# A transformer block in split fp32: seven-product blocks in two more places of the MLP, two quarters of a gate moved beside them, its first loads moved forward

## The chip, the cores and the metric

The kernel runs on one core of a Trainium2 chip. The time is that of one execution on the device in microseconds (us), from the first to the last instruction and what lies around them. Lower is better. Names used below: PE is TensorE (matrix products), PEld its weight loads, DVE is VectorE, ACT ScalarE, POOL GpSimd, SP the engine that issues most of the loads.

## The reference

One layer is computed for 128 context tokens and 256 latent tokens, 384 in all, at width 2048:

```python
shift_a, scale_a, gate_a, shift_f, scale_f, gate_f = mod     # silu(cond) @ ada_w + ada_b, cond is c_ctx or c
h = rmsnorm(x, norm_w[0]) * (1 + scale_a) + shift_a
q, k, v, o, g, u = split(h @ w_in)
hm = rmsnorm(mlstm_bidir(q, k, v, g + gate_bias, C0, n0, m0)) * sigmoid(o)   # 8 heads x 128, chunks of 128
hp = pool_mixer(u)                                           # 4 groups x 256
x = x + gate_a * rmsnorm(concat(hm, hp) @ w_out, norm_w[1])
h = rmsnorm(x, norm_w[2]) * (1 + scale_f) + shift_f
y = square(relu(h @ w1)) @ w2                                # 2048 -> 8192 -> 2048
x = x + gate_f * rmsnorm(y, norm_w[3])
```

Outputs are y for both token groups and the final mLSTM state of the context scan.

## The kernel before, in words

All products are in fp32 made of three matmuls: each operand is split into a rounded part hi and the rest lo, and hi·hi, hi·lo and lo·hi are summed in one PSUM bank. A weight slab (128 x 1024 numbers, 512 KB) is loaded by SP (`load_w`, L119), ACT copies it to hi (L131), DVE subtracts to get lo (L132), PE multiplies (`mm3`, L140 to L142).

The stages follow each other on PE: adaLN products and the input projection (0 to 205 us), q/k with attention, gates and pooling beside them (to 430), o (to 490), w_out (to 630), the norm r1 and the vector gate_f's first part (to 641), and then the MLP in eight chunks of eight hidden tiles each. Beside the large products run generators that a `Feed` (L147) steps: each call of a feed adds its rate to a sum and takes one step of the generator when the sum reaches one. `gemm_T` (L163) calls its feeds once per weight slab. A planner orders PE, DVE and ACT instructions by what they wait for, in order of the program for equal ones; a few stretches are in written order (`manual_schedule`).

The six modulation vectors come from 2048 x 12288 weights `ada_w`. Some columns go through PE (`ada_mat`, L208: matmuls of 32 x 256), others through DVE (`ada_vec`, L252): 32 multiply-and-add instructions per 512 columns over slabs `ada_raw`, line L273 (the first pair L271), then a small matmul sums over partitions. In w_out the generator `mid_vec` (L681) does five vectors of 1024 columns in this way. gate_f (`gate_f`, L839) has its first quarter done by `ada_mat` in the stretch between w_out and w1, where PE would wait for the norm (`fill`, L859); half of those weights go through the tiles y0 and y1, which are not yet in use. Its other three quarters follow by `ada_vec` at rate RATE_GF beside chunks 0 and 1.

In the MLP a `w1_group` (L1148) makes two hidden tiles: 96 matmuls of 384 columns. They are evacuated by `evac_normed` (L810) or `evac_pair` (L818). Then w2 follows. There are two forms. `mlp_out` (L935) does a block of 512 output columns n with 8 hidden tiles x 3 token tiles x 3 matmuls = 72 matmuls of 512 columns. `mlp_seven` (L1060) does the same block with seven products in place of eight for each 2 x 2 block of (hidden tile, token tile) and column half, after Winograd's scheme: 132 matmuls of 256 columns for the block, for which `evac_pair` builds sums of hidden tiles (s, hs) and DVE sums and splits weight slabs (L1077 and L1107 to L1121). Two of the products go into sums of their own, r16 and r7, over the chunks, and `seven_done` (L1135) adds these to y at the end of chunk 6. Before the change chunks 2 to 6 are done by `mlp_seven`, chunks 0, 1 and 7 by `mlp_out`. The last block of chunk 7 and the final norm, gate and residual stand in `last_part` (L1035), with `done` (L1014) for the squares and the gate.

## Time and profile before

| | |
|---|---|
| median of 3 runs | 1716.28 us (1715.2 to 1723.14) |
| the profiled execution's own time | 1715.41 us |
| its span, first to last instruction | 1713.4 us |
| mean granted TensorE clock | 0.995 of 2.4 GHz |
| PE / DVE / ACT / POOL busy | 98% / 75% / 42% / 9% of the span |
| DMA | 320.88 MB, mean 187 GB/s |

All times of views below are those of the profiled execution, counted from its first instruction. A share of busy time is an average over stages: which engine sets the pace has to be read stage by stage, from the waits of PE and from windows.

### The profile page before, as it was taken

How to read it: one execution, taken by the hardware profiler on the slowest of the kernel's cores; microseconds unless marked ns; L12 is line 12 of the kernel's file. 1: busy time of each engine (PE TensorE's matmuls, PEld its weight loads, DVE VectorE, ACT ScalarE, POOL GpSimd, SP SyncE). 2: the span in 40 equal slices, each digit the busy share in tenths (PEclk: the TensorE clock that was granted, in tenths of full speed). 3: DMA queues.
4: the chain of work that ended last, by engine and by line, in shares of the span. 5: the costliest groups of instructions: out<-in, count | busy, mean ns of one | idle time of the engine just before them, and what ended most of it. 6: DMA issues, size and time to landing. Idle time of an engine off the chain costs nothing.

```text
span 1713.4 us, 27071 instructions
## 1 busy us (share of the span) xinstructions
PE 1673.3 (98%) x10661; PEld 1567.0 (91%) x10661; DVE 1284.6 (75%) x1900; ACT 721.9 (42%) x1178; POOL 150.3 (9%) x186
## 2 busy tenths in 40 slices
...
GB/s 301 306 278 282 295 145 261 235 238 238 220 232 268 260 275 143 208 173 181 213 172 123 148 136 121 139 131 112 152 126 112 158 121 113 161 108 98 265 137 106
DMA packets 255758, 320.88 MB, mean 187 GB/s; under 512 B 14368, under 2 KB 218768, under 8 KB 255248
## 3 DMA queue, kind: packets, MB, share of 16 engines
...
q8 instruction: 83, 1.36, 0.3%
...
HBM read 308.61 MB, written 10.51 MB: 186 GB/s over the span
## 4 chain that ended last, share of the span: by engine, by line
PE 85%; DVE 6%; DMA 5%; issue 2%; ACT 1%; SPq 1%; POOL 0%; DVEq 0%; ACTq 0%; POOLq 0%
PE acc_w L140 10%; PE acc_w L141 10%; PE acc_w L142 10%; PE y L932 4%; PE y L931 3%; PE y L933 3%; PE y L1089 3%; PE y L1090 3%; PE y L1088 3%; DVE ada_acc L273 2%; DMA raw_u<-in_w_in_dram 2%; PE acc_wo L140 2%; PE acc_wo L142 2%; PE acc_wo L141 2%; PE y_yz L1089 2%
## 5 line engine op out<-in xcount | busy, mean ns | idle before, releaser
L132 DVE TENSOR_TENSOR lo_w<-raw_w,hi_w 128x1024 fp32r<-128x1024 f32 x176 | 215.2, 1224 | 192.9 <-ACT hi_w L131 191.0
L141 PE MATMUL acc_w<-h2l,hi_w 128*128 128x384 f32 (+1 forms) x1024 | 345.6, 338 | 0.5 <-DVE h2l L887 0.5
L142 PE MATMUL acc_w<-h2h,lo_w 128*128 128x384 f32 (+1 forms) x1024 | 344.8, 337 | 0.0
L140 PE MATMUL acc_w<-h2h,hi_w 128*128 128x384 f32 (+1 forms) x1024 | 343.8, 337 | 1.1 <-ACT h2h L883 0.6
L131 ACT ACTIVATE hi_w<-raw_w 128x1024 fp32r<-128x1024 f32 x176 | 186.5, 1060 | 304.3 <-PE acc_w L141 97.2
L273 DVE SCALAR_TENSOR_TENSOR ada_acc<-ada_raw,sg,ada_acc 128x1024 f32<-128x1024 f32 (+1 forms) x240 | 258.8, 1116 | 1.3 <-DMA ada_raw<-in_ada_w_dram 1.3
L140 PEld LDWEIGHTS acc_w<-h2h,hi_w 128*128 128x128 f32 x1024 | 192.1, 188 | 2.7 <-ACT h2h L883 0.9
L141 PEld LDWEIGHTS acc_w<-h2l,hi_w 128*128 128x128 f32 x1024 | 192.6, 188 | 1.2 <-DVE h2l L887 0.8
L142 PEld LDWEIGHTS acc_w<-h2h,lo_w 128*128 128x128 f32 x1024 | 192.5, 188 | 0.1
L1076 ACT ACTIVATE hi_t<-w 128x1024 fp32r<-128x1024 f32 x80 | 84.4, 1061 | 87.2 <-PE y L1090 23.5
L1077 DVE TENSOR_TENSOR lo_t<-w,hi_t 128x1024 fp32r<-128x1024 f32 x80 | 97.4, 1223 | 11.7 <-ACT hi_t L1076 11.3
L1077 DVE TENSOR_TENSOR lo_b<-w,hi_b 128x1024 fp32r<-128x1024 f32 x60 | 73.3, 1222 | 35.3 <-ACT hi_b L1076 35.3
L1076 ACT ACTIVATE hi_b<-w 128x1024 fp32r<-128x1024 f32 x60 | 63.7, 1061 | 77.1 <-PE acc_w L141 51.3
L131 ACT ACTIVATE hi_wo<-raw_wo 128x1024 fp32r<-128x1024 f32 x32 | 34.1, 1064 | 75.2 <-DMA raw_wo<-in_w_out_dram 43.1
...
L226 PE MATMUL ada<-ada_raw,cT 128*32 128x256 f32 x672 | 47.6, 403 | 1.9 <-DMA ada_raw<-in_ada_w_dram 1.8
L399 PE MATMUL v<-hi_v,hh 128*128 128x384 f32 (+1 forms) x144 | 47.6, 332 | 0.0
L400 PE MATMUL v<-lo_v,hh 128*128 128x384 f32 (+1 forms) x144 | 46.5, 323 | 0.0
L401 PE MATMUL v<-hi_v,hl 128*128 128x384 f32 (+1 forms) x144 | 46.5, 323 | 0.0
L132 DVE TENSOR_TENSOR lo_wo<-raw_wo,hi_wo 128x1024 fp32r<-128x1024 f32 x32 | 40.2, 1270 | 7.3 <-ACT hi_wo L131 7.3
L140 PE MATMUL acc_k<-hh,hi_k 128*128 128x384 f32 x128 | 44.4, 347 | 1.2 <-ACT C L608 1.2
L140 PE MATMUL acc_q<-hh,hi_q 128*128 128x384 f32 x128 | 44.4, 347 | 0.0
...
## 6 DMA issues: line engine op xcount, KB each, us to landing
ada_raw<-in_ada_w_dram SPq DMA_DIRECT2D x188, 512.0 KB, 4.8
raw_w<-in_w_dram SPq DMA_DIRECT2D x176, 512.0 KB, 4.1
...
```

What stands on the lines that cost most here:

```text
L131: nc.scalar.activation(hi[:, 0:n], raw[:, 0:n], AF.Copy)
L132: low = lambda: nc.vector.tensor_tensor(lo[:, 0:n], raw[:, 0:n], hi[:, 0:n].bitcast(F32), op=ALU.subtract)
L140: nc.tensor.matmul(ps, lh, rh, start=start, stop=False)
L141: nc.tensor.matmul(ps, lh, rl, start=False, stop=False)
L142: mm3.ins = nc.tensor.matmul(ps, ll, rh, start=False, stop=stop).ins
L273: nc.vector.scalar_tensor_tensor(acc[:, g, :], raw[:, a, :], cj, acc[:, g, :], op0=ALU.mult, op1=ALU.add)
L931: nc.tensor.matmul(acc, xh[:, s], hi, start=k == 8 * ch, stop=False)
L932: nc.tensor.matmul(acc, xh[:, s], lo, start=False, stop=False)
L933: nc.tensor.matmul(acc, xl[:, s], hi, start=False, stop=k == 8 * ch + 7)
L1076: nc.scalar.activation(hi, raw, AF.Copy)
L1077: nc.vector.tensor_tensor(lo, raw, hi.bitcast(F32), op=ALU.subtract)
L1089: nc.tensor.matmul(acc, xh, wl, start=False, stop=False)
```

## The change

1. Chunk 1 goes by `mlp_seven` (S_FIRST 1), and so do the first two of the four blocks of chunk 7 (N_LAST 2). `evac_pair` serves all hidden tiles from 8 on. In chunk 7 the product x7's difference of hidden tiles is built by `evac_pair` as a tile d (one ACT copy and one more DVE subtraction per pair), and `seven_done` for the first two blocks runs as a feed beside the other two blocks.
2. Of gate_f's three `ada_vec` quarters one is left in chunk 0, at rate 0.4 in place of 0.65. The other two run beside chunks 1 and 2 at rate 0.25, with slabs of 256 KB and three buffers in place of 512 KB and four. `mlp_seven` steps the feed after each product of the second and third token tile.
3. Six of the eight loads for gate_f's first quarter go into y0, y1 and y2, and are issued during w_out (`early`). For this the MLP's pool is opened before w_out, and the pool of the ada slabs lies on the right side of SBUF.
4. The first chunk of the projection of u does all hi·hi, then all hi of the weight with lo of the tokens, then lo of the weight, and its weight's lo is subtracted after the token's lo.
5. The ACT copy `ada_sb` gets high priority. The Square of the head norm (L638) writes to an SBUF tile of its own in the cases where it wrote into a PSUM bank. The final gate is held in pieces of 384 columns. The buffers of z go from 5 to 4, the slots from 56 to 55, and the second raw pool's from 3 to 2.

```diff
-N_SLOT = 56
+N_SLOT = 55
 N_W = 4
 N_ADA = 4
 N_E = 1
 ADA_STEPS = (4, 0, 5, 0, 0)
 X_ORDER = "tatatatabtatatatat"
 N_X = 4
-RATE_GF = 0.65
-S_FIRST, S_LAST = 2, 6
+RATE_GF = 0.4
+RATE_GS = 0.25
+S_FIRST, S_LAST, N_LAST = 1, 6, 2
...
+                raw = raws.pop(0) if raws else None
+                if raw is None:
+                    raw = (wp if tag == "lo" else adap).tile([P, nj, w], F32, tag=tag, name=f"ada_raw_{i}_{k0}_{j0}", bufs=N_W if tag == "lo" else N_ADA)
+                    nc.sync.dma_start(raw, aw[:, j0:j0 + nj, c0:c0 + w])
...
-        sb = adap[0].tile([P, 512], F32, tag="adasb", name=f"ada_sb_{parts[0][0]}_{parts[0][1]}", bufs=1)
-        nc.scalar.activation(sb[:, 0:w], ps[:, 0:w], AF.Copy)
+        sb = adap.tile([P, 512], F32, tag="adasb", name=f"ada_sb_{parts[0][0]}_{parts[0][1]}", bufs=1)
+        with tc.high_priority():
+            nc.scalar.activation(sb[:, 0:w], ps[:, 0:w], AF.Copy)
...
+        acc = vec["acc"].tile([P, 2, n], F32, tag="adaacc", name=f"ada_acc_{i}_{c}", bufs=1)
+        c0, nj = i * D + c, vec["slab"] // n
 
         def load(t):
-            raw = adap[0].tile([P, nj, n], F32, tag="ada", name=f"ada_raw_{i}_{c}_{t}", bufs=N_ADA)
+            raw = vec["pool"].tile([P, nj, n], F32, tag="ada", name=f"ada_raw_{i}_{c}_{t}", bufs=vec["bufs"])
             nc.sync.dma_start(raw, aw[:, nj * t:nj * t + nj, c0:c0 + n])
             return raw
 
...
+            ways = ((0, 0), (1, 0), (0, 1))
+            for ps in [ways[n:n + 1] for n in range(3)] if s == ci == 0 else [ways]:
+                for k in range(nk):
+                    for i in range(3):
+                        for a, b in ps:
+                            nc.tensor.matmul(acc[i][:, 0:n], h[k0 + k][a][:, i * P:(i + 1) * P], (hi, lo)[b][:, k, :],
+                                             start=k == 0 and a + b == 0, stop=k == nk - 1 and b == 1)
+            if s == ci == 0:
+                w_first = load_chunk(0, 1, h_ins)
...
+                unread = (num if i > 0 else att.tile([P, 2, 129], F32, tag="num", name=f"sq_{hp}_{hl}", bufs=2))[:, 1, 0:128]
...
-                nc.scalar.activation(num[:, 1, 0:128] if i > 0 else ps[:, 260:388], hs[:, hl, :], AF.Square, accum_out=ssh[:, i, hd:hd + 1])
+                nc.scalar.activation(unread, hs[:, hl, :], AF.Square, accum_out=ssh[:, i, hd:hd + 1])
...
+    early = []
     for cols in ([0, 256], [512], [768], [1024], [1280], [1536], [1792]):
+        if cols[0] in (768, 1024, 1280):
+            for m in range(2):
+                n = len(early)
+                t = y[n // 2][:, 1024 * (n % 2):1024 * (n % 2) + 1024].rearrange("p (j c) -> p j c", c=256)
+                nc.sync.dma_start(t, aw[:, 4 * (n % 4):4 * (n % 4) + 4, 5 * D + 256 * (n // 4):5 * D + 256 * (n // 4) + 256])
+                early.append(t)
...
-        z = mlp.tile([P, NTOK], F32, tag="z", name=f"z{t}", bufs=5)
-        nc.scalar.activation(z, ps[:, 0:NTOK], AF.Relu)
+
+        z = relu_first(t, ps) if t < 10 else mlp.tile([P, NTOK], F32, tag="z", name=f"z{t}", bufs=4)
+        if t >= 10:
+            nc.scalar.activation(z, ps[:, 0:NTOK], AF.Relu)
         nc.scalar.activation(z, z, AF.Square)
         if t % 2 == 0:
             z_even.append(z)
             return
-        z0, s = z_even.pop(), mlp.tile([P, NTOK], F32, tag="z", name=f"s{t}", bufs=5)
+        z0, s = z_even.pop(), mlp.tile([P, NTOK], F32, tag="z", name=f"s{t}", bufs=4)
         a11, a21, a12, a22 = z0[:, P:2 * P], z0[:, 2 * P:], z[:, P:2 * P], z[:, 2 * P:]
         s1, s2, s4 = (s[:, i * P:(i + 1) * P] for i in range(3))
         tt = nc.vector.tensor_tensor
         tt(s1, a21, a22, op=ALU.add)
-        tt(a21, a11, a21, op=ALU.subtract)
+        if t < 8 * S_LAST + 8:
+            tt(a21, a11, a21, op=ALU.subtract)
+        else:
+            s3, d = mlp.tile([P, NTOK], F32, tag="z", name=f"d{t}", bufs=4), slot(f"hd{t}", F32R)
+            tt(s3[:, 0:P], a11, a21, op=ALU.subtract)
+            hi, lo = d[:, 0:P], d[:, P:2 * P]
+            nc.scalar.activation(hi, s3[:, 0:P], AF.Copy)
+            tt(lo, s3[:, 0:P], hi.bitcast(F32), op=ALU.subtract)
+            hid["d", t] = hi, lo
...
-        yield from ada_mat([(5, 0, 2), (5, 2, 2)], ("ada", None), [y[i][:, 1024 * n:1024 * n + 1024] for i in range(2) for n in range(2)])
+        yield from ada_mat([(5, 0, 2), (5, 2, 2)], raws=early)
         for q in (1, 2, 3):
-            yield from ada_vec(5, 512 * q, 512, adap[0])
+            yield from ada_vec(5, 512 * q, 512)
+            if q == 1:
+                vec["half"] = True
+                while vec["half"]:
+                    yield
...
+        for c, d in pieces:
+            lo, hi = max(a, c), min(b, d)
+            if lo < hi:
+                nc.vector.tensor_tensor(y[i][:, lo:hi], y[i][:, lo:hi], gf[min(i, 1), c][:, lo - c:hi - c], op=ALU.mult)
...
+                if m == "x7" and half and ch > S_LAST:
+                    xh, xl = hid["d", t + 1]
...
+            if tok:
+                for f in feeds:
+                    f()
...
     for ch in range(8):
         if ch < S_FIRST:
-            w1_group(4 * ch + 4, (ff, fx), 386 if ch == 0 else NTOK)
-            mlp_out(ch, (ff, fx, fn) if ch == 0 else (ff, fx))
-            if ch == 0:
-                fn.finish()
+            w1_group(4, (ff, fx), 386)
+            mlp_out(ch, (ff, fx, fn))
+            fn.finish()
+            for g in range(5, 8):
+                w1_group(g, (ff,))
+        elif ch <= S_LAST:
+            if ch == S_FIRST:
+                fx.finish()
+                while not vec.get("half"):
+                    next(ff.gen)
+                for scope in (xb_scope, acc_scope, ada_scope):
+                    scope.close()
+                str_scope = ExitStack()
+                strp = str_scope.enter_context(tc.tile_pool(name="strp", bufs=1, side="right", reuse_waits="tile"))
+                vec.update(pool=strp, acc=strp, slab=512, bufs=3, half=False)
+                ff.rate = RATE_GS
+                r16, r7 = strp.tile([P, 4, 512], F32, name="r16"), strp.tile([P, 4, 256], F32, name="r7")
+            for n in range(4):
+                mlp_seven(ch, n, strp, r16, r7, (ff,))
+                if n == 1:
+                    w1_group(4 * ch + 4, (ff,))
+            if ch == S_LAST:
+                ff.finish()
+                for n in range(N_LAST, 4):
+                    seven_done(n, r16, r7)
             for g in range(1, 4):
                 w1_group(4 * ch + 4 + g, (ff,))
...
-            ws = mlp_out(ch, (), done)
+            for n in range(N_LAST):
+                mlp_seven(ch, n, strp, r16, r7)
+
+            def done_late():
+                for n in range(N_LAST):
+                    seven_done(n, r16, r7)
+                    yield
+                    for i in range(3):
+                        done(i, 512 * n, 512 * n + 512)
+                        yield
+
+            fd = Feed(done_late(), 1.0)
+            ws = mlp_out(ch, (fd,), done, N_LAST)
+            fd.finish()
```

The first place in the order is DVE in chunk 0, around the lo of the weight slab of the block n = 2, hidden tiles 2 and 3 (lo_w2_2_2). ada_acc is gate_f's sum, h2n and h2l belong to the norm r2, x1b to the store of x. Before:

```order
L953 COPY y0_6318<-y_0_1_0_7616 128x512
L953 COPY y1_6319<-y_0_1_1_7617 128x512
L807 SCALAR_TENSOR_TENSOR h2l7_6640<-h2n7_7772,mod_118,h2h7_6639 128x128
L807 SCALAR_TENSOR_TENSOR h2l7_6640<-h2n7_7772,mod_118,h2h7_6639 128x256
L953 COPY y2_6320<-y_0_1_2_7618 128x512
L273 SCALAR_TENSOR_TENSOR ada_acc_5_512_7335<-ada_raw_5_512_6_7723,sg_111,ada_acc_5_512_7335 128x512 x4
L802 TENSOR_TENSOR h2n8_7815<-h2h8_6734,h2l8_6735 128x384
L132 TENSOR_TENSOR lo_w2_2_2_7825<-raw_w2_2_2_7822,hi_w2_2_2_7824 128x1024
```

After:

```order
L825 TENSOR_TENSOR h2n7_7771<-h2h7_6647,h2l7_6648 128x384
L133 TENSOR_TENSOR lo_w2_0_2_7787<-raw_w2_0_2_7784,hi_w2_0_2_7786 128x1024
L830 SCALAR_TENSOR_TENSOR h2l6_6631<-h2n6_7734,mod_118,h2h6_6630 128x128
L830 SCALAR_TENSOR_TENSOR h2l6_6631<-h2n6_7734,mod_118,h2h6_6630 128x256
L826 TENSOR_TENSOR h2n7_7771<-h2n7_7771,r2bc_6433 128x384
L825 TENSOR_TENSOR h2n8_7814<-h2h8_6742,h2l8_6743 128x384
L133 TENSOR_TENSOR lo_w2_2_2_7824<-raw_w2_2_2_7821,hi_w2_2_2_7823 128x1024
L933 STREAM_TRANSPOSE x1b15_7765<-mo15_6337 128x384
```

Before, four of gate_f's instructions stand in front of that lo; after, none of them does, and none stands between the lo of slab 0 of the block n = 1 and this one.

The second place is DVE in a first block (n = 0) of `mlp_seven`. lo_x_0_t1 is the lo of the third weight sum, z and s the last pair of hidden tiles and its sums, hidNNl the lo of a hidden tile. Before, in chunk 2:

```order
L1077 TENSOR_TENSOR lo_2_0_t1_9701<-w2_2_0_00_9599,hi_2_0_t1_9700 128x1024
L830 TENSOR_TENSOR s23_9576<-z22_9570,z23_9573 128x128
L831 TENSOR_TENSOR z22_9570<-z22_9570 128x128
L833 TENSOR_TENSOR s23_9576<-s23_9576,z22_9570 128x128
L834 TENSOR_TENSOR s23_9576<-z23_9573,s23_9576 128x128
L187 TENSOR_TENSOR hid22l_9580<-z22_9570,hid22h_9579 128x384
L187 TENSOR_TENSOR hid23l_9584<-z23_9573,hid23h_9583 128x384
L187 TENSOR_TENSOR hs23l_9590<-s23_9576,hs23h_9589 128x384
L1109 TENSOR_TENSOR y0_6318<-y_2_0_x7_9607,y0_6318 128x512
```

After, in chunk 1, the same work with gate_f's instructions between:

```order
L276 SCALAR_TENSOR_TENSOR ada_acc_5_1024_8566<-ada_raw_5_1024_4_9001,sg_111,ada_acc_5_1024_8566 128x512
L1156 TENSOR_TENSOR w2_1_0_10_8528<-w2_1_0_10_8528,w2_1_0_11_8530 128x1024
L1107 TENSOR_TENSOR lo_1_0_t1_8635<-w2_1_0_00_8526,hi_1_0_t1_8634 128x1024
L849 TENSOR_TENSOR s15_8501<-z14_8495,z15_8498 128x128
L276 SCALAR_TENSOR_TENSOR ada_acc_5_1024_8566<-ada_raw_5_1024_4_9001,sg_111,ada_acc_5_1024_8566 128x512
L851 TENSOR_TENSOR z14_8495<-z14_8495 128x128
L860 TENSOR_TENSOR s15_8501<-s15_8501,z14_8495 128x128
L276 SCALAR_TENSOR_TENSOR ada_acc_5_1024_8566<-ada_raw_5_1024_5_9158,sg_111,ada_acc_5_1024_8566 128x512
L188 TENSOR_TENSOR hid14l_8505<-z14_8495,hid14h_8504 128x384
L861 TENSOR_TENSOR s15_8501<-z15_8498,s15_8501 128x128
L188 TENSOR_TENSOR hid15l_8509<-z15_8498,hid15h_8508 128x384
L1144 TENSOR_TENSOR y0_5065<-y_1_0_x7_8534,y0_5065 128x512
```

One of them stands before the last weight sum, and two between lo_1_0_t1 and the lo of the hidden tiles 14 and 15; eight more stand before these rows in the block.

The third place is PE between w_out and w1. tr_r1 is the norm's bank: first the sums over partitions, and at last the matmul with dg_r1 that spreads the result. ada_5 is gate_f. Before:

```order
L782 MATMUL tr_r1_6358<-cst_72,sq_mo15_6305 128x1 x3
L226 MATMUL ada_5_0_6372<-ada_raw_5_0_0_6373,cT_109 32x256 x4
L226 MATMUL ada_5_0_6372<-ada_raw_5_0_4_6379,cT_109 32x256 x4
L226 MATMUL ada_5_0_6372<-ada_raw_5_0_8_6385,cT_109 32x256 x4
L226 MATMUL ada_5_0_6372<-ada_raw_5_0_12_6391,cT_109 32x256 x4
L201 MATMUL tr_r1_6358<-dg_r1_6397,cst_72 128x384
L226 MATMUL ada_5_0_6372<-y0_6318,cT_109 32x256 x8
L226 MATMUL ada_5_0_6372<-y1_6319,cT_109 32x256 x8
L140 MATMUL acc_w1_0_0_6426<-h2h0_6438,hi_w1_0_0_6434 128x386
```

After:

```order
L806 MATMUL tr_r1_6374<-cst_72,sq_mo15_6333 128x1 x3
L226 MATMUL ada_5_0_6388<-y0_5065,cT_109 32x256 x8
L226 MATMUL ada_5_0_6388<-y1_5066,cT_109 32x256 x8
L202 MATMUL tr_r1_6374<-dg_r1_6405,cst_72 128x384
L226 MATMUL ada_5_0_6388<-y2_5067,cT_109 32x256 x8
L226 MATMUL ada_5_0_6388<-ada_raw_5_2_8_6416,cT_109 32x256 x4
L226 MATMUL ada_5_0_6388<-ada_raw_5_2_12_6422,cT_109 32x256 x4
L141 MATMUL acc_w1_0_0_6434<-h2h0_6446,hi_w1_0_0_6442 128x386
```

Before, the matmuls ahead of the spread read four slabs that are loaded at that time; after, they read y0 and y1, and those behind it read y2 and two slabs. On SP the two loads of y0 and the first of y1 now stand right behind the fifth of the sixteen slabs ada_raw_3_1024, among the loads of raw_wo for w_out's first two column groups, the others a few rows on.

## Rows read from the trace of the kernel before

**Rows 1.** Busy time of each engine, whole kernel (page, part 1).
```profile
PE 1673.3 (98%) x10661; PEld 1567.0 (91%) x10661; DVE 1284.6 (75%) x1900; ACT 721.9 (42%) x1178; POOL 150.3 (9%) x186
```

**Rows 2.** Windows: busy us (x instructions) by engine, clock, DMA share, GB/s.
```profile
510.00:600.00 90.00, 89.02 (x512) 87.29 (x511) 89.02 (x72) 32.51 (x47) 20.75 (x11) 1.00 0.83 264
600.00:630.00 30.00, 30.00 (x177) 28.91 (x176) 16.98 (x22) 9.76 (x17) 10.57 (x18) 1.00 0.76 248
630.00:641.40 11.40, 10.23 (x86) 4.41 (x85) 4.37 (x14) 2.66 (x8) 0.88 (x1) 0.70 1.08 348
871.82:888.54 16.72, 16.72 (x73) 13.53 (x73) 16.72 (x27) 7.00 (x11) 0.00 (x0) 1.00 0.56 185
990.22:1005.79 15.57, 15.57 (x133) 15.57 (x133) 12.87 (x18) 10.53 (x16) 0.00 (x0) 1.00 0.45 136
1005.79:1021.37 15.58, 15.58 (x134) 15.58 (x133) 14.61 (x15) 8.10 (x10) 0.00 (x0) 1.00 0.45 135
1021.37:1038.13 16.76, 16.76 (x99) 16.76 (x98) 10.86 (x10) 4.94 (x6) 0.00 (x0) 1.00 0.41 127
```

**Rows 3.** Timeline, TensorE, chunk 0: start, us, instruction [idle before <-releaser].
```profile
772.17 0.50 PE L932 MATMUL y<-lo_w,hid2h 128*128 128x512 f32 x1 [3.05 <-DVE lo_w L132]
...
773.70 0.63 PE L931 MATMUL y<-hi_w,hid3h 128*128 128x512 f32 x1
...
777.07 0.39 PE L933 MATMUL y<-hi_w,hid3l 128*128 128x512 f32 x1
```

**Rows 4.** Timeline of VectorE at the same place.
```profile
767.78 2.73 DVE L273 SCALAR_TENSOR_TENSOR ada_acc<-ada_raw,sg,ada_acc 128x512 f32<-128x512 f32 x4
...
770.89 1.22 DVE L132 TENSOR_TENSOR lo_w<-raw_w,hi_w 128x1024 fp32r<-128x1024 f32 x1
```

**Rows 5.** Timeline of TensorE between w_out and w1.
```profile
632.19 2.03 PE L226 MATMUL ada<-ada_raw,cT 128*32 128x256 f32 x24
...
635.89 1.65 PE L201 MATMUL tr_r<-dg_r,cst 128*128 128x384 f32 x2
637.47 2.99 PE L226 MATMUL ada<-y,cT 128*32 128x256 f32 x24
...
641.43 0.81 PE L140 MATMUL acc_w<-h2h,hi_w 128*128 128x386 f32 x3
```

**Rows 6.** Timeline of VectorE in the same stretch.
```profile
633.66 0.56 DVE L199 TENSOR_TENSOR dg_r<-cst,r_r 128x384 f32<-128x384 f32 x1 [0.99 <-POOL r_r L193]
637.58 1.00 DVE L879 SCALAR_TENSOR_TENSOR mo<-mo,mod,tr_r 128x128 f32<-128x128 f32 x3 [3.36 <-PE tr_r L201]
```

**Rows 7.** Waits of TensorE, 20 to 205 us: total, times, longest.
```profile
PE ada L234 <- ACT ada_sb L231: 2.9, 4, 1.4
PE u L400 <- DVE lo_u L132: 1.4, 1, 1.4
```

**Rows 8.** Waits of TensorE, 370 to 440 us.
```profile
PE inter L628 <- ACT num L638: 2.5, 2, 1.3
```

**Rows 9.** Line 638, the Square: duration ns min/median/max of its instructions.
```profile
L638 ACT ACTIVATE num<-hs x8: 261/278/283, 288.3 to 436.1; 128x128 f32<-128x128 f32 x8
L638 ACT ACTIVATION_READ_ACCUMULATOR num<-hs x8: 187/189/198, 288.5 to 436.3; 128x1 f32 x8
```

**Rows 10.** Timeline of VectorE in the first quarter of chunk 2.
```profile
987.16 1.23 DVE L1077 TENSOR_TENSOR lo_b<-w,hi_b 128x1024 fp32r<-128x1024 f32 x1 [2.98 <-ACT hi_b L1076]
988.42 1.22 DVE L1117 TENSOR_TENSOR w<-w,w 128x1024 f32<-128x1024 f32 x1
...
994.40 0.55 DVE L187 TENSOR_TENSOR hid23l<-z,hid23h 128x384 fp32r<-128x384 f32 x1
```

**Rows 11.** Timeline of TensorE at the same place.
```profile
995.42 0.28 PE L1090 MATMUL y_yz<-hi_b,hid23l 128*128 128x256 f32 x1
```

**Rows 12.** Timeline of VectorE in the tail.
```profile
1700.36 0.69 DVE L1020 TENSOR_TENSOR y<-y,gf 128x512 f32<-128x512 f32 x1 [0.85 <-ACT jky L1018]
...
1702.27 0.43 DVE L1020 TENSOR_TENSOR y<-y,gf 128x256 f32<-128x256 f32 x1 [0.64 <-ACT jky L1018]
```

115 lines of the change are left out of this document (41 added, 74 removed).

## The prediction, written before the changed kernel had run

> **What bounds the kernel now.** I read the busy times first: PE is busy 98% of the span [rows 1], so the time can fall in two ways only: fewer or cheaper matmuls, or less of the 40 us in which PE stands (1713.4 less 1673.3), most of it at the start and in the tail. Then the windows stage by stage [rows 2]. In each, compare PE's busy time with its length, then look for an engine that is as full as PE. In the w2 blocks PE is never idle, in either form. DVE is full in w_out (89.02 of 90 us) and in a block of chunk 1 (16.72 of 16.72), and has slack in a w1 group (10.86 of 16.76). Then the waits and timelines at the few places where PE stands [rows 3, 5, 7, 8]. Each is a term below only if the change moves what it waits for.
>
> **Matmuls in chunks 1 and 7.** A block by `mlp_out` takes 16.72 us: 72 matmuls of 512 columns, 0.232 each. A block by `mlp_seven` takes 15.57 and 15.58: 132 of 256 columns, 0.118 each [rows 2]. That is 1.15 us less for each block, and half as wide a matmul costs hardly more per column (0.461 against 0.453 ns). Six blocks change, four in chunk 1 and two in chunk 7: 6 x 1.15 = 6.9 us less, all on PE's path, since PE has no idle time there. The windows are of PE at the full clock, so this term is sure as long as DVE and ACT keep up.
>
> **The stall in chunk 0.** PE waits 3.05 us for a weight's lo [rows 3]. DVE isn't idle then: the four instructions of gate_f ahead of that lo take 2.73 us [rows 4], and the order shows them there. Behind the wait the clock falls to half: eight matmuls from 773.70 to 777.07 take 3.37 us in place of 8 x 0.232 = 1.86, another 1.5. After the change, counted in the order, 12 instead of 23 of gate_f's instructions stand between the lo of the first slab of the block n = 0 and this lo: 11 x 0.68 (2.73 by four) is 7.5 us of DVE time, more than twice the wait. I take the whole stall away: -4.5. The ends are 0 (another lo is late in its place, since evacuations and the norm r2 have moved up) and -4.6.
>
> **Between w_out and w1.** Before, gate_f's matmuls in this stretch wait for slabs just loaded. dg_r1 is ready at 633.66 + 0.56 = 634.22 [rows 6], but the spreading matmul starts only at 635.89, w1 at 641.43 [rows 5]. The clock of the stretch is 0.70 [rows 2]. After, y0 and y1 are long loaded. The 32 records ahead of the spread (two for each matmul of the order) then take 32 x 0.085 (2.03 by 24) = 2.7 from 632.19: spread at 634.9, 1.0 earlier. With the distance of rows 5 and 6 (637.58 - 635.89 = 1.69) DVE starts x1 at 636.6, and the 32 records behind the spread, from 636.5 at the same 0.085 to 0.125 (2.99 by 24), end at 639.2 to 640.5. w1 would start around 639.4 in place of 641.43: -2.0. The ends are 0 (DVE, which makes h2 for w1's first three groups, is the pace there, and gives it back) and -3.6, if the clock stays full and the spread follows dg_r1 at once: 1.7 us earlier, and the records behind it at half the price save 1.9 more.
>
> On the clock the Trainium skill has a rule that bears on this stretch ("TensorE: Matmul & The Clock Gate", section "Why this matters for your kernels"): idle gaps between bursts of matmuls bring the clock down to half. The two falls above agree (0.70 in this stretch; half behind the 3.05 us wait). By it the changed stretch, in which PE still waits for the norm, falls again, which goes with -2.0 rather than -3.6.
>
> **Small waits.** In the first chunk of u PE waits 1.4 for lo_u [rows 7]; the new order puts twelve matmuls (2.8 us) between, but lo_u now stands behind the tokens' lo on DVE, and what follows is fed by loads. I take -0.6 (0 to -1.4). The waits of `inter` for the Square are 2.5 in two [rows 8]. The bank comes free one Square and its read earlier, 0.278 + 0.187 = 0.47 each [rows 9], so -0.9 for the two (0 to -2.5). ada_sb: PE waits 2.9 in four for it [rows 7]. The order of ACT's instructions around ada_sb is the same in both programs, so the new priority does nothing and the waits stay: 0. If it did what it says, -2.9.
>
> **What the change adds: gate_f beside the seven products.** A block by `mlp_seven` holds eleven DVE instructions of 128 x 1024 at 1.26 (987.16 to 988.42 [rows 10]), 13.9 us, and adds of y: about 16 with nothing else, so DVE lives on the slack of the w1 groups, 5.9 us in one [rows 2]. Into the blocks n = 0 and 1 come 14 of gate_f's instructions, into n = 2 and 3 13: 27 x 0.68 = 18 us. They can be done ahead, as far as buffers go: in chunk 2 DVE waited 2.98 us for ACT just before the first weight sums [rows 10], so part of the nine that stand before lo_1_0_t1 falls into idle time. But two stand directly ahead of the lo of tiles 14 and 15. The counterpart in chunk 2, hid23l, is done at 994.40 + 0.55 = 994.95 and read at 995.42 [rows 10, 11]: 0.47 us of slack. Two instructions are 1.36, so PE stands about 0.9 there. The block n = 2 needs no hidden tile anew, and its weights are split ahead during the w1 group. I take +1.5 for the chunk. The lower end is 0, as DVE does all of it early; the upper +3.6, when of the nine 5.7 us only 2.98 is covered, so 2.7 late, plus 0.9. Behind a late lo on DVE stand the adds that free PSUM banks, and PE waits for those too. The two groups of w1 in chunk 2 that take most of the last quarter have the slack for it: 0.
>
> **The rest.** In the tail the gate's multiply is cut at the pieces: two of 256 take 2 x 0.43 against 0.69 in one [rows 12], 0.17 for each of the cut ones; some are behind a wait for ACT. +0.3 (0 to +1.0). x7's d in chunk 7 costs DVE 4 small instructions where it has slack, and `seven_done` runs beside full PE blocks: 0. The pools, z with four buffers, and slots: loads into them wait for reads that are long past, 0; if four z buffers held up `evac_pair`, it would show as PE waiting for hidden tiles.
>
> **Sum.** -6.9 - 4.5 - 2.0 - 0.6 - 0.9 + 1.5 + 0.3 = -13.1, from the execution's own 1715.41: 1702.3. The median of the runs is 0.87 above that execution, so 1703.2; I say 1703. All good ends together give -6.9 - 4.6 - 3.6 - 1.4 - 2.5 = -19, so 1697; all bad ends -6.9 + 3.6 + 1.0 = -2.3, so 1714.
>
> **Rivals.**
>
> *DVE becomes the bound of chunk 1, and the kernel is slower.* The place is DVE in the four blocks, the price the 18 us of gate_f. It decides when the weights of a block can't be split ahead (three raw buffers and two of the second pool), so that nothing of it is hidden. Then +18 takes the place of +1.5, and if the four blocks stand some 4.5 us each, each stand is followed by half clock, as the 3.05 us wait was, at 1.5 each: +24. 1715.41 - 14.6 + 24 + 0.87 = 1725.7. For it: DVE's 16.72 of 16.72 in chunk 1 before. Against it: in that block, which held gate_f's instructions too, PE was not idle for a moment, so the buffers carried it. 5%.
>
> *The stall in chunk 0 stays or moves to another lo.* The sum of DVE's work in chunk 0 falls only by what is moved out. If the first two blocks hold as much as now, by the norm r2 and the store of x moved up, PE stands elsewhere: 1703.2 + 4.5 = 1707.7, and 1709 if another wait follows. For it: DVE has no idle time before that wait [rows 4]. Against: 7.5 us are taken out for a wait of 3. 16%.
>
> *The early loads hold up w_out.* Six loads of 512 KB, 3.1 MB, stand on SP ahead of slabs of ada_raw and raw_wo, while DVE is full. At 264 GB/s and 0.83 share the engines could move 318 GB/s [rows 2], so one load is 1.65 us, and three in a row hold back what stands behind them by 4.9. DVE then idles up to 4.9, and PE waits for lo_wo: 1703.2 + 4.9 = 1708.1. Against: in the last 30 us of w_out DVE is busy 16.98 only [rows 2], so work pushed back finds room there. 12%.
>
> The Trainium skill states for it ("DMA: Bandwidth & Descriptors", section "Queues, rings and completion order") that each DMA engine takes the descriptors of an issuing engine's ring in order. By that an early load is in the way of all that SP issues after it, which is what this rival needs; no row of before has such loads in a full stretch.
>
> The forecast keeps 67%.
>
> **How the numbers follow.** A measurement of this kernel can tell about 0.5% from no change, 8.6 us: faster means below 1707.7, slower above 1724.9. The forecast's own range is 1699 to 1707, nearly all of it faster (0.65); the second and third rival lie on the limit, half of each below it (0.13). Faster 0.78, within 0.5% 0.17, slower 0.05. For 8 in 10 I take 1698 to 1710: it holds the forecast and the two rivals at the limit, and leaves out the slower one and the ends at which several terms go one way.
>
> **What would show it.** Blocks of chunk 1 and the first two of chunk 7 at 15.6 us of PE each; no wait of PE for a lo_w in chunk 0, and full clock there; the first w1 matmul 7.2 us after the last sum of the norm in place of 9.2; in chunk 1 a wait of PE for hid14l or hid15l of about 1 us in the first block and little else; the waits for ada_sb unchanged; DVE in w_out still full and lo_wo waited for no longer than before. The prediction is wrong if PE's windows in chunk 1 are longer than 16.7 per block, if a stall of over 3 us stands anywhere in chunk 0, or if w_out grows.

## The result, and the profile after

The changed kernel takes 1708.85 us (median of five runs, 1705.35 to 1710.82), the kernel before 1717.49 beside it: ratio 0.9944, with an interval of 0.9924 to 0.9963. A second set of runs gave 0.9946 (0.9931 to 0.9960). So 9 us are gone where 13 were forecast. The profiled execution took 1710.82, its span is 1709.0.

Busy time of each engine in the changed kernel (the counterpart of [rows 1]):

```profile
PE 1670.3 (98%) x11021; PEld 1585.8 (93%) x11021; DVE 1342.1 (79%) x2000; ACT 750.1 (44%) x1224; POOL 154.7 (9%) x194
```

PE's busy time has fallen by 3.0 only, though the change takes out 6.9 us of matmuls by the prediction's count. That sum mixes two parts. Ahead of the first sums of the norm behind w_out, where executions differ by several us, PE is busy 4.5 us longer in this profile than in the one of before (609.8 against 605.4); behind them it is busy 7.4 us less (1060.5 against 1067.9). Even 7.4 is less than the 6.9 of the blocks, the 1.5 of half clock in chunk 0 and the 3.5 of PE's busy time in the stretch before w1 (10.23 to 6.72) make together, so some matmuls have become dearer, which the sum didn't have. Busy time by stage shows where (columns as in [rows 2]):

```profile
510.00:600.00 90.00, 89.08 (x511) 87.35 (x511) 88.99 (x74) 30.09 (x46) 16.24 (x9) 1.00 0.84 276
600.00:636.60 36.60, 36.60 (x214) 35.51 (x213) 23.27 (x26) 12.52 (x18) 14.28 (x20) 1.00 0.92 303
636.60:644.00 7.40, 6.72 (x86) 4.16 (x85) 3.25 (x11) 2.44 (x9) 0.88 (x1) 1.00 0.19 61
766.39:783.07 16.68, 16.68 (x73) 13.53 (x72) 16.68 (x31) 7.23 (x12) 0.54 (x1) 1.00 0.47 142
851.47:867.19 15.72, 15.72 (x134) 15.68 (x134) 15.67 (x24) 10.47 (x16) 0.00 (x0) 1.00 0.57 182
867.19:882.81 15.62, 15.62 (x135) 15.62 (x134) 15.54 (x17) 7.56 (x9) 0.00 (x0) 1.00 0.42 125
899.64:915.49 15.85, 15.85 (x134) 15.71 (x132) 15.85 (x23) 10.68 (x16) 0.00 (x0) 1.00 0.53 161
915.49:932.69 17.20, 16.71 (x135) 15.88 (x134) 16.32 (x18) 7.14 (x9) 0.00 (x0) 1.00 0.44 135
983.29:998.96 15.67, 15.67 (x134) 15.67 (x133) 12.93 (x19) 10.03 (x14) 0.00 (x0) 1.00 0.43 135
1471.19:1488.01 16.82, 16.82 (x98) 16.82 (x97) 7.48 (x11) 7.18 (x12) 0.00 (x0) 1.00 0.41 124
1634.60:1650.20 15.60, 15.60 (x134) 15.60 (x133) 13.04 (x21) 10.78 (x17) 2.51 (x5) 1.00 0.68 224
```

Read them from above. The first two are the end of w_out: VectorE (DVE) full as before. The third is the stretch from the norm's sums behind w_out to w1, called the fill here: 7.40 us at the full clock, 11.4 at 0.70 before [rows 2]. The fourth is the block of chunk 0 that had the stall: 16.68. The next four are chunk 1, the first of chunk 2 follows; in chunk 1 only the last one is far from 15.6, and DVE is full or nearly so in all four. The last two are a w1 group (16.82, where [rows 2] has 16.76), and a block of chunk 7.

The fill in detail, on TensorE (the counterpart of [rows 5]; start, us, instruction [idle before <-releaser]):

```profile
638.60 1.93 PE L226 MATMUL ada<-y,cT 128*32 128x256 f32 x32
640.69 0.91 PE L202 MATMUL tr_r<-dg_r,cst 128*128 128x384 f32 x2 [0.15 <-DVE dg_r L200]
641.53 1.07 PE L226 MATMUL ada<-y,cT 128*32 128x256 f32 x16
642.42 1.05 PE L226 MATMUL ada<-ada_raw,cT 128*32 128x256 f32 x16
644.00 0.80 PE L141 MATMUL acc_w<-h2h,hi_w 128*128 128x386 f32 x3 [0.53 <-ACT h2h L910]
```

No wait for a transfer is left. The 32 records ahead of the spread take 1.93 us (2.03 for 24 in [rows 5]), and those behind it 2.1 in place of 3.6. w1 starts 5.40 us after the last norm sum (644.00 - 638.60) in place of 9.24.

Waits of TensorE, 20 to 210 us, then 370 to 440 (total, times, longest), the counterparts of [rows 7, 8]:

```profile
PE ada L235 <- ACT ada_sb L232: 3.6, 4, 1.3
PE ada L226 <- DMA ada_raw<-in_ada_w_dram: 0.7, 2, 0.4
...
PE inter L635 <- DVE hs L645: 0.8, 1, 0.8
...
PE inter L635 <- DVE C L618: 0.6, 1, 0.6
```

The wait for lo_u is gone, `inter` no longer waits for the Square but still waits, and ada_sb is waited for four times as before (3.6 us against 2.9). One more reading needs the whole trace: the time from the fill to the end is 1083.1 and 1081.4 in two profiled executions of the kernel before, and 1072.4, 1073.2, 1073.0 and 1073.6 in four that issue the changed kernel's instructions in its order. That is 9.2 less (1082.25 against 1073.05), and in it each stage repeats to a few tenths. Ahead of the fill it doesn't: 630.2 and 634.4 us before, 631.9 to 636.6 after. So the experiments are read from the fill on, stage by stage; the times of whole runs stand beside.

### The profile page after: what moved, and what is told of

Read it like the earlier page. It is cut to its first block, busy times and chain, and to the rows that moved or that the text cites. A ratio compares the mean times of both kernels' runs of the same rounds, so it can differ in the third digit from the quotient of the medians.

```text
span 1709.0 us, 28009 instructions
## 1 busy us (share of the span) xinstructions
PE 1670.3 (98%) x11021; PEld 1585.8 (93%) x11021; DVE 1342.1 (79%) x2000; ACT 750.1 (44%) x1224; POOL 154.7 (9%) x194
## 4 chain that ended last, share of the span: by engine, by line
PE 79%; DVE 8%; DMA 6%; issue 4%; ACT 1%; POOL 1%; SPq 1%; DVEq 0%; ACTq 0%; POOLq 0%
PE acc_w L141 9%; PE acc_w L142 9%; PE acc_w L143 9%; PE y L1121 4%; PE y L1122 4%; PE y L1120 4%; PE v L405 3%; PE u L405 2%; PE y_yz L1120 2%; PE y_yz L1121 2%; PE y_yz L1122 2%; PE acc_wo L141 2%; PE acc_wo L143 2%; PE acc_wo L142 2%; DVE ada_acc L276 2%
## 5 line engine op out<-in xcount | busy, mean ns | idle before, releaser
L133 DVE TENSOR_TENSOR lo_w<-raw_w,hi_w 128x1024 fp32r<-128x1024 f32 x152 | 185.3, 1221 | 136.2 <-ACT hi_w L132 135.9
L132 ACT ACTIVATE hi_w<-raw_w 128x1024 fp32r<-128x1024 f32 x152 | 160.8, 1058 | 214.2 <-PE acc_w L142 93.9
L1106 ACT ACTIVATE hi_t<-w 128x1024 fp32r<-128x1024 f32 x104 | 109.5, 1060 | 117.7 <-DVE w L1142 33.0
L1107 DVE TENSOR_TENSOR lo_t<-w,hi_t 128x1024 fp32r<-128x1024 f32 x104 | 126.4, 1221 | 14.9 <-ACT hi_t L1106 14.6
L1107 DVE TENSOR_TENSOR lo_b<-w,hi_b 128x1024 fp32r<-128x1024 f32 x78 | 95.2, 1222 | 39.0 <-ACT hi_b L1106 38.7
L1106 ACT ACTIVATE hi_b<-w 128x1024 fp32r<-128x1024 f32 x78 | 82.5, 1060 | 96.7 <-PE acc_w L142 64.1
L840 ACT ACTIVATE z<-acc_w 128x384 f32<-128x384 f32 x54 | 26.3, 487 | 75.1 <-PE acc_w L143 75.1
```

The lines of the kernel that those rows point to most:

```text
L132: nc.scalar.activation(hi[:, 0:n], raw[:, 0:n], AF.Copy)
L133: low = lambda: nc.vector.tensor_tensor(lo[:, 0:n], raw[:, 0:n], hi[:, 0:n].bitcast(F32), op=ALU.subtract)
L1106: nc.scalar.activation(hi, raw, AF.Copy)
L1107: nc.vector.tensor_tensor(lo, raw, hi.bitcast(F32), op=ALU.subtract)
```

## The experiments

The first two runs repeat the changed kernel and the kernel before.

> The changed kernel, unaltered, a second time. The profiled execution of it was the slowest of its five (1710.82 us, median 1708.85) and that of before the fastest but one (1715.41, median 1717.49). Theory A: about 4 us of what is missing against the forecast lie in these two executions and not in the kernels. Then this trace is nearer 1707, the wait of DVE for the store of C in the q/k stage (1.8 us, line 618) and the half clock behind it do not come back, and a w1 group of 96 matmuls is nearer 16.75 than 16.82 us. Theory B: the change itself brought them. Then both are there again at the same places, and the time is 1709 to 1711. Ratio to before 0.992 to 0.996 by both.

> The kernel before, unaltered, for a second trace. Theory A: its matmul period can be as long as that of the changed kernel's first trace (a w1 group 16.82 in place of 16.75 us), its time between 1715 and 1720, and the stall in chunk 0 (3.05 us, line 932) is there again, since the order makes it. Theory B: the w1 group is 16.75 again, and only the changed kernel has 16.82.

Measured: 1709.17 (ratio 0.9946) and 1717.87. Theory B holds for the w1 groups in both: 16.82 again in the changed kernel, 16.75 again in the kernel before. The wait of VectorE for the store of C came back too (1.6 us), but it stands in the second profile of before as well (1.2), so it isn't the change's; no half clock followed it this time. The stall of chunk 0 came again in the kernel before, but smaller: its third block took 21.04, against 22.82 in the first profile. PE waited 2.3 for the same lo, and no half clock followed. The changed kernel's chunk 0 has four blocks of 16.6 to 16.7 in both.

**Chunk 1 by three products again.** The gate's feed there goes back to 0.65, w1's next group stands ahead of the blocks, and `mlp_out` does them:

```
             if ch == S_FIRST:
+                ff.rate = 0.65
+                w1_group(4 * ch + 4, (ff,))
+                mlp_out(ch, (ff,))
...
-    k0, c0, first = 8 * ch, 512 * n, ch == S_FIRST
+    k0, c0, first = 8 * ch, 512 * n, ch == S_FIRST + 1
```

> The changed kernel with chunk 1 by mlp_out again (the hidden tiles 8 to 15 without the sums, gate_f's feed at rate 0.65 in that chunk); all else as changed. Theory A (a seven-product block is 1.15 us less on PE, and gate_f beside it costs next to nothing): 4.6 us slower than the changed kernel, 1713 to 1714, and the four w2 blocks of chunk 1 take 66.9 us of PE in place of 62.7. Rival (DVE sets the pace of chunk 1 in the changed kernel): at most 2 us slower.

Measured: 1711.94, ratio to the kernel before 0.9958 (0.9942 to 0.9974), 2.8 above the changed kernel. In the trace the four blocks take 66.8 us; in the four executions of the changed program 64.4, 65.0, 64.8 and 65.5. So the seven products bring 1.9 in chunk 1, where -4.6 + 1.5 = -3.1 was forecast. The blocks of three products cost what the theory said, but the seven products' blocks don't reach its 62.7; at 1.9 by the trace the rival is nearer.

**Without the gate's last two quarters.** They are left out of the computation, their rows set to 1:

```
-            yield from ada_vec(5, 512 * q, 512)
+            if q == 1:
+                yield from ada_vec(5, 512 * q, 512)
+            else:
+                nc.vector.memset(mod[:, 5, 4 * q:4 * q + 4, :], 1.0)
```

> The changed kernel without gate_f's quarters 2 and 3: their loads, their 64 DVE instructions and their 24 small matmuls are left out, and the gate's columns are set to one. Theory A (the DVE work is hidden): 2.2 us faster than the changed kernel, which are the 24 small matmuls of 1.1 us a quarter, and no more than 0.5 us besides. Rival (gate_f's DVE work holds up PE by 1.5 us or more in chunks 1 to 3): 4 us faster or more, and the blocks of chunk 1 get shorter by that.

Measured: 1703.55, ratio 0.9916 (0.9887 to 0.9945), so the quarters cost 5.6. The last block of chunk 1 without them:

```profile
914.77:930.41 15.64, 15.64 (x134) 15.64 (x133) 15.61 (x16) 7.57 (x9) 0.00 (x0) 1.00 0.36 107
```

It is 15.64 in place of 17.20, and chunk 1 takes 62.6 in all, 1.8 to 2.8 less than with them. Another 2.4 are the quarters' 24 small matmuls in chunks 2 and 4, which the kernel before has too, in other places, and 1.0 comes from the other blocks, which take 15.57 here in place of 15.63. The rival holds: over 4 in all, and the blocks of chunk 1 are shorter by more than 1.5. Theory A, the work hidden to within 0.5, fails.

**Chunk 7 by three products again.** `N_LAST` 0 in place of 2.

> The changed kernel with the three products back in the first two column blocks of chunk 7 (the seven products end with chunk 6). In the changed kernel's profile these two blocks took 15.60 and 15.63 us where the kernel before had 16.70 and 16.69. Theory (a block costs its matmuls, 84 products of 256 columns against 72 of 512): both blocks are back at 16.7, the tail behind them stays as it is, and the kernel is 2.1 us slower than the changed one, about 1711. Rival (part of the gain is given back behind the blocks, because the sums of the seven products have to be finished beside the last two blocks, where VectorE writes the result): the blocks go back to 16.7, but the last two blocks and the tail get shorter, and the kernel is less than 1.2 us slower.

Measured: 1713.0, ratio 0.9962 (0.9947 to 0.9978). (A block by seven products has 132 matmuls of 256 columns, not the 84 named.) Its two blocks are back at 16.73 each, so 2.2 us, and the rest of the tail is the same within 0.1. The runs differ by more than that, 4; in this execution chunk 1 also took 66.3, 0.8 above the highest of the four. The theory holds for the blocks.

**The early loads, moved.** The six loads are taken out of w_out's loop and written behind it.

> The changed kernel with the six early loads of gate_f's first quarter moved from within w_out to behind it; everything else as in the changed kernel. Theory (the fill between w_out and w1 is shorter because ada_w's rows already lie in SBUF, which keeps TensorE going and its clock at 2.4 GHz): the fill is 11.2 to 11.6 us again as in the kernel before, in place of 7.4, with waits for DMA within the 32 matmuls of the gate and a stretch at the half clock behind them, and the kernel is 4 us slower, about 1713. Rival (it is shorter because the buffers of the MLP no longer wait for other pools to be given back, and the early loads only come along): the fill stays under 8.5 us and the time within 1 us of the changed kernel's.

Measured: 1707.08, fill 7.39. But this tells nothing: the scheduler put the loads where they had been, and every engine's order is that of the changed kernel. The run counts as one more of it. A second try ties them to VectorE:

```
+    for n in range(6):
...
+        with tc.issue_after(load_w.lo):
+            nc.vector.memset(t[:, :, 0:1], 0.0)
+        nc.gpsimd.dma_start(t, aw[...])
```

> The changed kernel with the six early loads of gate_f's first quarter (3 MB) moved out of w_out: they are issued by GpSimd's queue, behind small memsets of their tiles that stand on VectorE behind the last low part of w_out, some 10 us ahead of the fill. Theory (the fill between w_out and w1 got shorter because these rows already lie in SBUF): the transfers land while the fill runs, its 32 matmuls of the gate wait for DMA again, TensorE loses its clock behind them, and the fill takes 10 to 12 us in place of 7.4; the kernel is 3 to 4 us slower. Rival (the fill got shorter because the pools are opened early, and no longer wait for others to be given back): the fill stays under 8.5 us, and the time within 1 us of the changed kernel's.

Measured: 1717.0, ratio 1.0004; the fill took 17.23. TensorE and GpSimd in it:

```profile
635.47 1.93 PE L226 MATMUL ada<-y,cT 128*32 128x256 f32 x32
645.75 1.65 PE L202 MATMUL tr_r<-dg_r,cst 128*128 128x384 f32 x2 [8.35 <-DVE dg_r L200]
647.33 1.94 PE L226 MATMUL ada<-y,cT 128*32 128x256 f32 x16
```

```profile
621.04 4.50 POOL L797 DMA_DIRECT2D y<-in_ada_w_dram  x6 [4.04 <-DVE y L796]
...
643.67 0.54 POOL L883 DMA_DIRECT2D xTr<-xT_dram  x1 [0.51 <-issue]
644.22 0.88 POOL L194 TENSOR_TENSOR r_r<-r_r,mhalf 128x3 f32<-128x3 f32 x1
```

The number agrees with neither theory, and the reason is another one. The gate's matmuls at 635.47 didn't wait: their rows had landed. What waited is the spread of the norm, 8.35 us, for one instruction of 0.88 on GpSimd (POOL), the norm's power. That stood behind sixteen loads of x, and these behind the six. The loads had been moved to POOL's queue, and the norm runs through that queue. So the place of the loads isn't tested by itself; that the waits for transfers left with them is read from the two traces alone.

**The rate that fed chunk 0.** `RATE_GF` 0.65 in place of 0.4.

> The changed kernel with the rate of gate_f's feed up to chunk 0 back at 0.65 (in the changed kernel 0.4). Its second quarter's 32 steps on VectorE then stand earlier in chunk 0's column blocks. Theory (that rate caused the stall of the kernel before, where the third block of chunk 0 took 22.8 us in place of 16.7, because VectorE came late with a low part of w2): the third or fourth block gets longer again by 3 to 6 us, with PE waiting for a low part on VectorE, and the kernel is 3 to 6 us slower, about 1713. Rival (the stall came from transfers that the pools' old order made wait, so that it doesn't return): chunk 0's blocks stay at 16.7, and the time within 1 us of the changed kernel's.

Measured: 1708.76, ratio 0.9954 (0.9940 to 0.9969). The stall is back in the third block (20.89; some 2 of the 4.2 over 16.68 lie at a quarter's small matmuls, the rest at the stall), at its first lo; TensorE, then VectorE:

```profile
767.17 0.50 PE L963 MATMUL y<-lo_w,hid0h 128*128 128x512 f32 x1 [1.91 <-DVE lo_w L133]
```

```profile
764.70 1.28 DVE L984 COPY y<-y 128x512 f32<-128x512 f32 x2
765.90 1.22 DVE L133 TENSOR_TENSOR lo_w<-raw_w,hi_w 128x1024 fp32r<-128x1024 f32 x1
767.03 2.74 DVE L276 SCALAR_TENSOR_TENSOR ada_acc<-ada_raw,sg,ada_acc 128x512 f32<-128x512 f32 x4
```

DVE has no gap over 0.2 in the 20 us up to that lo. So the rate set the stall, as the theory said. Yet the time is the changed kernel's, not the 1713 of the theory: with the quarter done earlier, chunk 1 takes 62.6 (four blocks of 15.6), and no small matmuls stand in the w1 groups ahead of it. So 0.4 in place of 0.65 moved a cost from chunk 0 to chunk 1 and won little by itself: 1073.05 from the fill on, against 1073.7.

**The late quarters where VectorE has room.** Their steps are fed only in the three w1 groups behind the blocks of chunks 1 to 3, each queued on VectorE behind that group's lo. Nothing is left out.

```
-RATE_GS = 0.25
+RATE_GS = 1.0
...
+    def gate_step():
+        late[0] = load_w.lo
+        ff()
...
-                mlp_seven(ch, n, strp, r16, r7, (ff,))
+                mlp_seven(ch, n, strp, r16, r7)
...
-                w1_group(4 * ch + 4 + g, (ff,))
+                w1_group(4 * ch + 4 + g, (gate_step,))
```

> The changed kernel with quarters 2 and 3 of gate_f's product with a vector moved out of chunk 1's column blocks: its steps on VectorE stand in the three w1 groups behind the blocks of chunks 1, 2 and 3, in order behind these groups' own low parts. Nothing is left out. Theory (in chunk 1 these steps delay the low parts for the seven products, 1.8 to 2.4 us, most of it in the last block): the four blocks of chunk 1 take 15.6 to 15.7 us each, the w1 groups 16.8 or up to 18 where the quarter's own 12 small matmuls stand, and the kernel is 2 us faster than the changed one, about 1707. Rival (the steps cost what they cost wherever they stand, because VectorE has no room behind the blocks either): the w1 groups in which they stand get longer by 0.5 us each, and the time stays within 1 us of the changed kernel's.

Measured: 1706.47, ratio 0.9931 (0.9914 to 0.9948); 1071.0 from the fill on, 2.1 less. Blocks 0, 2 and 3 of chunk 1 and two w1 groups behind them:

```profile
851.53:867.13 15.60, 15.60 (x133) 15.60 (x133) 11.17 (x16) 10.46 (x16) 0.00 (x0) 1.00 0.44 135
899.63:915.29 15.66, 15.66 (x134) 15.66 (x133) 11.52 (x17) 10.49 (x16) 0.00 (x0) 1.00 0.44 135
915.29:930.93 15.64, 15.64 (x135) 15.64 (x133) 15.64 (x17) 7.58 (x9) 0.00 (x0) 1.00 0.34 106
930.93:947.77 16.84, 16.84 (x99) 16.84 (x98) 13.99 (x19) 5.65 (x6) 0.00 (x0) 1.00 0.91 296
947.77:964.58 16.81, 16.81 (x98) 16.81 (x97) 12.59 (x19) 7.17 (x12) 0.00 (x0) 1.00 0.61 191
```

The blocks are at 15.6, and the two groups hold twelve and eight of the gate's instructions at no cost. The theory holds.

**The seven products in three blocks of chunk 7**, on top of that.

```
-S_FIRST, S_LAST, N_LAST = 1, 6, 2
+S_FIRST, S_LAST, N_LAST = 1, 6, 3
...
-            for n in range(N_LAST):
+            for n in range(2):
                 mlp_seven(ch, n, strp, r16, r7)
...
+            mlp_seven(ch, 2, strp, r16, r7, (fd,))
```

> The kernel with gate_f's late quarters in the w1 groups behind the blocks of chunks 1 to 3 (1706.5 measured), and with the seven products in three of chunk 7's four column blocks in place of two. Theory (a block on seven products costs its matmuls, 15.65 us in place of 16.70, wherever VectorE keeps up): the third block of chunk 7 takes 15.65 and the kernel is 1 us faster, about 1705.5, the fastest of all. Rival (VectorE then has the sums of three blocks and the scaled residual's steps to do beside the last block, and is late at the end): the last block and the tail get longer by 1 to 4 us, and the kernel is not faster than without it, 1706.5 to 1710.

Measured: 1717.39, ratio 1.0003: the rival, and dearer than it said, 11 us. The block before the new one, the new one, and the stretch behind it:

```profile
1649.55:1665.18 15.63, 15.63 (x135) 15.63 (x133) 15.63 (x18) 6.58 (x7) 0.00 (x0) 1.00 0.40 121
1665.18:1684.60 19.42, 16.90 (x135) 16.04 (x133) 19.42 (x32) 9.08 (x14) 1.07 (x2) 1.00 0.27 91
1684.60:1701.20 16.60, 13.56 (x51) 10.78 (x50) 13.99 (x30) 6.22 (x14) 0.00 (x0) 0.79 0.09 32
```

DVE is busy for all of 19.42 us, since the finished blocks' sums and their gate stand between the parts of the third. A wait of 3.0 for a lo at 1688.27 follows, and half clock behind it (0.79). There is what the first rival of the prediction feared for chunk 1; it is real, but at the end. The edit also lets the sums of the first two blocks (`fd`) run beside the third; whether the third block would pay with these sums behind it was not run.

**Where the operands lie.** In the changed kernel the w1 groups from the sixth on take 16.82 in place of 16.75 where nothing else stands in them, and most blocks take some hundredths more, the same in every profiled execution. Two runs move tiles in SBUF and leave the work alone: one shifts the weight buffers and all slots by 128 bytes (a tile of that size ahead of them), one takes five slots out ahead of w1, so that the normalised input and what follows lie in other slots.

```
+    for i in range(5):
+        nc.gpsimd.memset(slot(f"spare{i}")[:, 0:2], 0.0)
     sqb = slot("sqb")
```

> The changed kernel with an unused tile of 128 bytes per partition ahead of one of the constants, which shifts the weight buffers and the slots of the operands by 128 bytes in SBUF; nothing else differs. In the kernel before, a w1 group of 96 matmuls of 384 columns takes 16.75 us, in the changed kernel 16.82, in each of its executions and also where chunk 1 is undone. Theory (the place of the operands in SBUF sets it: the change took 2432 bytes out of the pool in front of them): the group's time is a third number, or 16.75 again, apart from 16.82 by 0.03 us or more, and the blocks of the seven products move with it; if it is 16.75 the kernel gains 2 to 3 us. Rival (what else runs beside the matmuls sets it, such as the longer use of the right side's pool): 16.82 as before, and the time the same within 1 us.

> The changed kernel with five unused tiles taken from the slots ahead of w1, so that the 32 tiles of the normalised input (and what follows) lie in other slots in SBUF. Every engine issues the same instructions in the same order as the changed kernel; only addresses differ. With all tiles shifted alike by 128 bytes, a w1 group of 96 matmuls kept its 16.82 us. Theory (the period of a matmul depends on where its operands lie relative to each other, and the changed kernel's slots happen to be the slower ones): the group's time is another one, 16.7 to 16.9 but not 16.82, the same in every group of the MLP, and the time moves by 32 times the difference; each of the 32 moving tiles has another mean period than in the changed kernel. Rival (what is issued beside the matmuls sets it, or the buffers of the weights, which haven't moved): 16.82 as before, and the same pattern over the 96 matmuls.

Measured: 1708.44, ratio 0.9945 (0.9929 to 0.9960), and 1706.21, ratio 0.9946 (0.9933 to 0.9958). One w1 group of 96 matmuls, in the kernel before, then shifted by 128 bytes, then with five slots taken (the changed kernel's stands above, 1471.19):

```profile
1474.10:1490.85 16.75, 16.75 (x98) 16.75 (x97) 7.47 (x11) 7.18 (x12) 0.00 (x0) 1.00 0.43 125
```

```profile
1470.68:1487.50 16.82, 16.82 (x97) 16.82 (x97) 7.47 (x11) 7.18 (x12) 0.00 (x0) 1.00 0.42 123
```

```profile
1470.37:1487.10 16.73, 16.73 (x97) 16.73 (x97) 7.48 (x11) 7.19 (x12) 0.00 (x0) 1.00 0.41 122
```

The same DVE and ACT work beside them, the full clock, no idle time: 16.75, 16.82 and 16.73. A shift of everything by 128 bytes changes nothing (the first run's rival), other slots for the operands change all groups (16.73 to 16.76; the second run's theory), and chunk 0's blocks from 16.68 to 16.58, with the order of all engines the same but for five memsets on POOL. So it is where the operands lie, and not what runs beside. Whether their distance from the weight buffers counts, which stayed in place, or an address of their own in steps below 128 bytes, is not told apart: five slots are no whole number of 128 bytes. The blocks of chunks 2 to 6 did not come back: without those that hold small matmuls their mean is 15.58 before, 15.63 in the changed kernel and 15.63 here. From the fill on this kernel takes 1070.2, 2.8 less than the changed one: 2.1 in the w1 groups, 0.3 in chunk 0, and the rest in chunk 1, which varies by more than that. The ratio of the whole runs doesn't show it, its interval is 2 us to either side.

## Why the prediction was right, and where its sum was off

The time came out inside the 8 in 10 range (1698 to 1710), on the side forecast, but above the forecast's own 1699 to 1707 and 6 us above the value given. By its own steps, from the traces:

| step | forecast, us | measured, us |
|---|---|---|
| six blocks on seven products | -6.9 | -6.4 |
| the gate beside them in chunk 1 | +1.5 | +1.8 to +2.8 |
| the stall in chunk 0 | -4.5 | -4.9, -3.1 |
| between w_out and w1 | -2.0 | -3.9, -4.2 |
| u -0.6, `inter` -0.9 | -1.5 | none seen |
| tail | +0.3 | +0.1 |
| matmuls dearer elsewhere | not in the sum | +2.7 |

The measured steps add up to some -9.2, the difference from the fill on. Part of the hit is luck: the fill gave 2 us more than the sum had, and without them the time would be about 1711, outside the range.

*The blocks.* In chunk 7 16.70 + 16.69 became 15.60 + 15.63, so -2.2. In chunk 1, with the gate out of the way, 62.6 against 4 x 16.71 = 66.8, so -4.2. Right; the 0.5 that is missing is mostly the dearer matmul of the last line.

*The gate in chunk 1.* The mechanism was right, the size a little low, the main place missed. The prediction looked for a wait of 1 us for hid14l and hid15l in the first block. There is one, at hid14h: 0.1 us in the first profile, 0.2 to 0.5 in the three others with this order. In the second profile (VectorE, ScalarE, TensorE) one of the gate's instructions stands ahead of the tile's square:

```profile
855.12 0.74 DVE L276 SCALAR_TENSOR_TENSOR ada_acc<-ada_raw,sg,ada_acc 128x512 f32<-128x512 f32 x1
855.78 0.28 DVE L851 TENSOR_TENSOR z<-z 128x128 f32<-128x128 f32 x1
856.10 0.52 ACT L187 ACTIVATE hid14h<-z 128x384 fp32r<-128x384 f32 x1 [2.23 <-DVE z L851]
856.67 0.39 PE L1120 MATMUL y_x<-hi_b,hid14h 128*128 128x256 f32 x1 [0.26 <-ACT hid14h L187]
```

Most of the loss is in the last block, 1.6 of its 17.20 (17.2 to 17.5 in all four), at four low parts of w2 that came late one after the other. TensorE, and VectorE beside it, in the first profile:

```profile
915.87 0.39 PE L1121 MATMUL y_x<-lo_b,hid8h 128*128 128x256 f32 x1
...
922.11 0.39 PE L1121 MATMUL y_yz<-lo_b,hid9h 128*128 128x256 f32 x1 [0.28 <-DVE lo_b L1107]
...
929.52 0.39 PE L1121 MATMUL y<-lo_t,hs9h 128*128 128x256 f32 x1
```

```profile
913.93 0.75 DVE L276 SCALAR_TENSOR_TENSOR ada_acc<-ada_raw,sg,ada_acc 128x512 f32<-128x512 f32 x1
914.59 1.23 DVE L1107 TENSOR_TENSOR lo_b<-w,hi_b 128x1024 fp32r<-128x1024 f32 x1
915.73 0.75 DVE L276 SCALAR_TENSOR_TENSOR ada_acc<-ada_raw,sg,ada_acc 128x512 f32<-128x512 f32 x1
916.39 1.23 DVE L1107 TENSOR_TENSOR lo_b<-w,hi_b 128x1024 fp32r<-128x1024 f32 x1
918.50 1.23 DVE L1142 TENSOR_TENSOR w<-w,w 128x1024 f32<-128x1024 f32 x1 [0.88 <-DMA w<-in_w_dram]
```

Each of the three matmuls is the first to read a low part, and starts 0.3 to 0.6 behind the one before it, where 0.118 is usual. On DVE the gate's instructions stand between the low parts without a gap through the third block (n = 2); a late slab of w2 adds 0.88. The working ahead was done, and used up by the last block (n = 3): the prediction priced n = 0, held n = 2 free because its weights are split ahead, and had nothing for n = 3. One of its own signs of being wrong was met there: a block over 16.7. The four blocks together stay under four times that (64.4 to 65.5).

*The stall.* Gone, as forecast; the rate's run brought it back. The third block fell by 6.1 and 4.3 from the two profiles of before, of which 1.2 are a quarter's small matmuls that now stand in a w1 group (17.95 for 16.82). But this term and the one above hang together, which the sum didn't see: at the old rate the stall costs some 3 in chunk 0, and chunk 1 is 2.4 shorter.

*The fill.* The traces fit the mechanism: no wait for a transfer is left (0.7 and 0.4 before). No run isolates it, as the early loads and the early pools were not parted. The size was half: the end named for the case that the clock stays full, -3.6, is what came. The rule cited from the Trainium skill ("TensorE: Matmul & The Clock Gate", section "Why this matters for your kernels") was taken to mean that the clock falls again. It didn't: 1.00, with 0.7 us of idle time in 7.40, and so in all profiles with the early loads; before, 0.70 and 0.71 stood beside 1.2 and 1.4 in 11.4 and 11.6 [rows 2]. The section speaks of longer gaps than any in this stretch (0.66 at most), so it bears neither on the fall before nor on the full clock after, and what decides between them here stays open. Behind the 8.35 us of the loads' second try the trace agrees with it: a granted clock of 0.53, and 16 records took 1.94, against 1.07 at the full clock.

*The small waits.* The wait for lo_u went, and nothing came of it that can be seen: q starts at 205.6 and 208.9 in the two profiles of before, and at 205.8 to 212.8 in twelve of kernels with the new order. `inter` waits 1.4 and 1.1 in the two profiles of the changed kernel, 2.8 and 2.9 before, in a part of the kernel that varies by 4 us. So these waits are shorter by more than forecast, and whether the time follows isn't seen.

*The dearer matmuls* are what the sum lacked. The prediction priced blocks and groups at the old kernel's matmul, and took the pools and one slot less as free. In the changed kernel 27 w1 groups take 0.07 more each, 20 blocks that were not touched 0.05, and chunk 0's are 0.04 shorter: +2.7. That the operands' places can do this is shown by the run that moved the slots, for the w1 groups (1.9 of the 2.7) and for chunk 0; which part of the change moved them, the missing slot or the pools, was not run. For the blocks of chunks 2 to 6 (1.0) the cause stays open: the moved slots left them at 15.63 and the gate's other place at 15.62; only without the quarters and their slabs they are at 15.57.

The rivals: the stall did not stay; the early loads did not hold up w_out (141.75 us in place of 141.51, and DVE full as before), though the Trainium skill's rule of one ring in order ("DMA: Bandwidth & Descriptors", section "Queues, rings and completion order") made that possible, and no run shows its price here; and VectorE was the bound of chunk 1 for 2 us, not for 24.

What stays open besides: which relation of addresses makes a matmul dearer (the mean by moving tile lies between 0.172 and 0.181 us in the changed kernel); whether the part ahead of the fill changed by less than 3 us; and the kernel with both the moved quarters and the other slots, some 2 us each by their traces, which was not run.
